# Weights and weight sums of the first up tiles made during the output projection of a diffusion layer

## The chip, the cores and the metric

The kernel runs on one core of a Trainium2 chip. The metric is the device time of one execution in microseconds (us); the time of a kernel is the median of its runs. The engines of the core are named as in the profile: PE (matrix products), DVE (vector), ACT (scalar functions and copies), POOL (GpSimd, elementwise work here) and SP (its queue issues the loads and stores).

## What is computed

One layer of a transformer for 128 context tokens and 512 latent tokens, model width 1024. The stretch that matters runs from the end of the mixer to the first up tiles of the channel sub-layer:

```python
x = x + ga * _merge(pool, na, gp, gn, w_pool_proj, w_na_proj, w_o)   # ends with (...) @ w_o
h = _modulated_norm(x, norm_ffn_g, sf, cf)
x = x + gf * _conv_ffn(h, w_up, ffn_conv_w, ffn_conv_b, w_down)

def _conv_ffn(h, w_up, conv_w, conv_b, w_down):
    u = h @ w_up
    up = jnp.pad(u, ((0, 0), (1, 1), (0, 0)))
    u = up[:, :-2] * conv_w[0] + up[:, 1:-1] * conv_w[1] + up[:, 2:] * conv_w[2] + conv_b
    a, g = jnp.split(u, 2, axis=-1)
    return (jax.nn.silu(a) * g) @ w_down
```

## The kernel before

**Arithmetic.** Every float32 operand of a product is split into a rounded high part and a remainder (split_to, L132: a cast on ACT, a subtraction on DVE), and each product is made of three matmuls, high by high, high by low and low by high. A weight tile is loaded into a buffer named raw (three of them, L125), and split into one of two pairs whi and wlo of the pool wp (L138).

**Output projection.** The mixer's result stands as mhi and mlo for five token tiles of 128. The first half of the 1024 columns is made for all five tiles at once (L718 to L722), the second half tile by tile (out_product, L730), from weights w1h and w1l that are split beforehand. residual (L708) then multiplies by the gate on DVE (L711, into one of two buffers o_t), adds to x1 (first half on POOL, L713; second half on DVE, L715) and sums the squares on ACT (L716). After the second half of a tile, out_product takes the root (L744), scales the row to xn (L747; two buffers xn2) and hands xn to second_h (L753): eight transposes on PE into small PSUM tiles sm, four modulated copies on ACT and four on DVE into hf (L764, L767), and the split into b1h, b1l, b12h, b12l, b2h, b2l. The program asks for the transposes of a tile in the middle of the next tile's out_product.

**Up projection.** It uses sums of quarters of weights and of h (seven products in place of eight). sums (L787) makes the sums of h on DVE for a range of columns J; split_sums (L796) splits them into th and tl; POOL makes the four sums of a weight tile (L859 to L862) in a buffer ws. Tile f = 0 is done without sums, by plain (L899), from the weights w0. For each later f, up_a makes two products from plain weights, up_w splits the weight sums, and products_b (L877, called in up_b) makes the other five products. up_a and up_w of tile f + 1 stand around up_b of tile f.

**Order.** A scheduler orders the instructions of each engine when the program is built: among those that it takes to be ready it prefers what stands earlier in the program. Each engine then runs its own list strictly in that order, waiting where data is late. Pools opened at L814 and L817 (tp, fw) take the memory of mhi, mlo, w1h and w1l, and so can be written only when the last output product is over. In the program the stretch ends like this:

```python
    w0a, rg = load_w(A["wup"][0]), load_raw(A["wup"][NF])
    ...                         # output projection; sums J[0] after tile 3, J[1] after tile 4
    hi, lo = [fw.tile([P, 1024], F32R, tag=x, name=x, bufs=1) for x in ("whi2", "wlo2")]
    split_to(rg, hi, lo)
    plain(B11, B21, HB, 1)
    second_h(4, xns[4])
    up_a(1)
    plain(B12, B22, H2C, 1 + HB)
    sums(*J[2])
```

B11 and B21 are the columns 0 to 321 of h, which end inside token tile 2; B12 and B22 are the rest, which need tile 4.

Of the kernel before, what the change touches and what calls it, by code (L numbers as in the profile page):

```python
# [10 lines left out]
F32 = mybir.dt.float32  # L11
F32R = mybir.dt.float32r
# [5 lines left out]
P = 128  # L18
D = 1024
# [45 lines left out]
def body(ctx, tc, A):  # L65
# [58 lines left out]
    def load_raw(src, tp=None):  # L124
        r = (tp or wp).tile([P, 1024], F32, tag="raw", name="raw", bufs=SRAW if tp else 3)  # L125
        dma = nc.sync.dma_start(r, src)
        if tp or pinned[0] > 0:
            tc.keep_in_program_order(dma)
            pinned[0] -= 0 if tp else 1
        return r  # L130

    def split_to(raw, hi, lo):  # L132
        nc.scalar.copy(hi, raw)  # L133
        nc.vector.tensor_tensor(out=lo, in0=raw, in1=hi.bitcast(F32), op=SUB)  # L134
# [297 lines left out]
    def to_grid_order(fn, ctx_dst, lat_dst, ps):  # L432
# [3 lines left out]
        fn(d[:, 0:3], blocks(ps[0][:, SEQ:320]))  # L436
        fn(d[:, 3:8], blocks(ps[1][:, :320]))

    def tanh_half(dst, src):
        i = nc.scalar.activation(dst, src, AF.Tanh, scale=0.5).ins  # L440
# [210 lines left out]
    def merge(i):  # L651
# [13 lines left out]
        nc.scalar.activation(mh, ta, AF.Copy, scale=0.5)  # L665
        nc.vector.scalar_tensor_tensor(out=ml, in0=ta, scalar=0.5, in1=mh.bitcast(F32), op0=MULT, op1=SUB)

    for i in range(KT):
        merge(i)
        for _ in range(2):  # L670
            next(mods, None)
        if i + 5 < KT:
            t2s[i + 5] = gate_na(i + 5)
# [34 lines left out]
    def residual(ps, t, chunk, sq):  # L708
        sl = slice(chunk * 512, (chunk + 1) * 512)
        tmp = fp.tile([P, 512], F32, name="o_t", bufs=2)  # L710
        nc.vector.tensor_tensor(out=tmp, in0=ps, in1=gab[:, 1 if t == 0 else 0, sl], op=MULT)  # L711
        if chunk == 0:
            nc.gpsimd.tensor_tensor(out=x1[:, t, sl], in0=x1[:, t, sl], in1=tmp, op=ADD)  # L713
        else:
            nc.vector.tensor_tensor(out=x1[:, t, sl], in0=x1[:, t, sl], in1=tmp, op=ADD)  # L715
        nc.scalar.activation(tmp, x1[:, t, sl], AF.Square, accum_out=sq[:, t:t + 1])  # L716
# [13 lines left out]
    def out_product(t, mid):  # L730
        ps = ps_acc()
        for kt in range(KT):
            if kt == MID and t:
                mid(t - 1)
            xh, xl = mhi[:, kt, tok_cols(t)], mlo[:, kt, tok_cols(t)]
            nc.tensor.matmul(ps, lhsT=xh, rhs=w1h[:, kt, :], start=(kt == 0), stop=False)
            nc.tensor.matmul(ps, lhsT=xh, rhs=w1l[:, kt, :], start=False, stop=False)
            nc.tensor.matmul(ps, lhsT=xl, rhs=w1h[:, kt, :], start=False, stop=(kt == KT - 1))
        residual(ps, t, 1, sq1)

        nc.sync.dma_start(xscr[:, t, :], x1[:, t, :])
        std = fp.tile([P, 1], F32, name="std2", bufs=2)
        nc.vector.tensor_tensor(out=std, in0=sq0[:, t:t + 1], in1=sq1[:, t:t + 1], op=ADD)
        nc.scalar.activation(std, std, AF.Sqrt, bias=eps, scale=1.0 / D)  # L744
        nc.vector.reciprocal(std, std)
        xn = fp.tile([P, D], F32, name="xn2", bufs=2)
        nc.scalar.activation(xn, x1[:, t, :], AF.Copy, scale=std)  # L747
        return xn

# [37 lines left out]
    def sums(j0, j1):  # L787

        b11, b21 = hf[:, 0:4, j0:j1], hf[:, 4:8, j0:j1]
        b12, b22 = hf[:, 0:4, HB + j0:HB + j1], hf[:, 4:8, HB + j0:HB + j1]  # L790
        nc.vector.tensor_tensor(out=b11, in0=b12, in1=b11, op=SUB)
        nc.vector.tensor_tensor(out=b12, in0=b22, in1=b12, op=SUB)
        nc.vector.tensor_tensor(out=b22, in0=b22, in1=b11, op=SUB)
        nc.vector.tensor_tensor(out=b21, in0=b21, in1=b22, op=SUB)
# [7 lines left out]
    J = ((0, 64), (64, 192), (192, HB))  # L802


    w0a, rg = load_w(A["wup"][0]), load_raw(A["wup"][NF])
    xns = []
    for t in range(5):
        xns.append(out_product(t, lambda t: second_h(t, xns[t])))
        if t >= 3:
            sums(*J[t - 3])  # L810
    e5.close()
    ex.close()
    e6 = ExitStack()
# [26 lines left out]
    def halves_of(w):  # L840
        return [tuple(x[:, i * 512:(i + 1) * 512] for x in w) for i in range(2)]
# [2 lines left out]

    def up_a(f):

        ra, rg = load_raw(A["wup"][f]), load_raw(A["wup"][NF + f])
        a11, a12, a21, a22 = ra[:, :512], ra[:, 512:], rg[:, :512], rg[:, 512:]
        hi, lo = [wp.tile([P, 1024], F32R, tag=x, name=x, bufs=2) for x in ("whi", "wlo")]
# [8 lines left out]
        s = fw.tile([P, 4, 512], F32, name="ws", bufs=1)  # L858
        nc.gpsimd.tensor_tensor(out=s[:, 1], in0=a21, in1=a22, op=ADD)  # L859
        nc.gpsimd.tensor_tensor(out=s[:, 0], in0=s[:, 1], in1=a11, op=SUB)  # L860
        nc.gpsimd.tensor_tensor(out=s[:, 2], in0=a11, in1=a21, op=SUB)
        nc.gpsimd.tensor_tensor(out=s[:, 3], in0=a12, in1=s[:, 0], op=SUB)  # L862
        ups[f] = pa, s, a22

    def up_w(f):

        pa, s, a22 = ups.pop(f)
        w = []
        for tp_, src, n in ((fw, s[:, 0:2].rearrange("p a b -> p (a b)"), 1024),
                            (wp, s[:, 2:4].rearrange("p a b -> p (a b)"), 1024), (fw, a22, 512)):  # L870
            e = "" if tp_ is wp else "2" if n == 1024 else "3"
            hi, lo = [tp_.tile([P, n], F32R, tag=x + e, name=x + e, bufs=2 if tp_ is wp else 1) for x in ("whi", "wlo")]
            split_to(src, hi, lo)
            w += halves_of((hi, lo)) if n == 1024 else [(hi, lo)]
        ups[f] = pa, w

# [15 lines left out]
        nc.scalar.copy(ug[:, h1], pa[:, cs])  # L892


    hi, lo = [fw.tile([P, 1024], F32R, tag=x, name=x, bufs=1) for x in ("whi2", "wlo2")]
    split_to(rg, hi, lo)
    w0 = [halves_of(w0a), halves_of((hi, lo))]

    def plain(x1_, x2_, n, c0):  # L899
        for (wa, wb), u in zip(w0, (us["a"][0], us["g"][0])):  # L900
# [3 lines left out]
            nc.scalar.copy(u[:, c0:c0 + n], ps[:, :n])  # L904

    plain(B11, B21, HB, 1)
    second_h(4, xns[4])
    up_a(1)
    plain(B12, B22, H2C, 1 + HB)
    sums(*J[2])  # L910
    for j in ((0, 192), (192, HB)):
        split_sums(*j)
    up_w(1)
# [206 lines left out]
```

## Time and profile before

| what | us |
|---|---|
| median of three runs | 908.28 |
| lowest and highest run | 905.41 and 909.32 |
| profiled execution, its own time | 908.53 |
| span of the profiled execution | 906.7 |
| PE busy in the span | 869.7 |
| DVE busy in the span | 669.9 |
| ACT busy in the span | 394.6 |
| POOL busy in the span | 232.9 |

The span runs from the first to the last instruction; the profiled time is 1.8 us longer. All places in the trace are given in us from the start of the span. The last output product ends near 450, and the up projection fills the rest of the span.

### The profile page before, as it was taken

Reading aid. Unit: us, or ns where it says so; the run is one execution under the profiler, and the core shown is the slowest. Engines: PE = TensorE matmul, PEld = TensorE weight load, DVE = VectorE, ACT = ScalarE, POOL = GpSimd, SP = SyncE. Lnnn points to the kernel's source line nnn. Section 1 sums busy time; section 2 is a strip of 40 time slices with the busy share of each in tenths; the row PEclk is TensorE's granted clock in tenths of the full one; section 3 lists DMA queues with packets and bytes.
Section 4 is the critical chain, followed back from the end, with each engine's and each line's share of the span. In section 5 each row is a group of like instructions: output and inputs, shape, how many; then the busy total and the mean of one; then the engine's idle time right before and its main releaser. Section 6 shows DMA issues by size and latency. Waiting matters only on the chain.

```text
span 906.7 us, 13346 instructions
## 1 busy us (share of the span) xinstructions
PE 869.7 (96%) x5234; PEld 781.0 (86%) x5234; DVE 669.9 (74%) x1000; ACT 394.6 (44%) x710; POOL 232.9 (26%) x179
## 2 busy tenths in 40 slices
PE   4999999999999999999979999999999999999997
PEld 3778897887889999987779898999999899999885
DVE  3656987897489633545699978879797887979767
ACT  5342245445453322224766444526354353544540
POOL 2220000000000021322115543354342345433304
PEclk9999999999999999999989999999999999999999
DMA  9958326573364222254123322212232221322206
GB/s 265 323 211 249 114 76 206 177 232 116 97 207 157 78 80 74 70 215 172 79 92 105 117 70 93 94 47 93 70 117 68 73 93 47 106 83 93 94 0 198
DMA packets 33023, 112.20 MB, mean 124 GB/s; under 512 B 3856, under 2 KB 4528, under 8 KB 32704
## 3 DMA queue, kind: packets, MB, share of 16 engines
q1 hardware_dynamic: 31840, 107.91, 35.8%
q0 software_dynamic: 1120, 3.44, 1.3%
q8 instruction: 41, 0.67, 0.3%
q14 instruction: 22, 0.18, 0.1%
HBM read 104.50 MB, written 5.78 MB: 122 GB/s over the span
## 4 chain that ended last, share of the span: by engine, by line
PE 77%; DVE 9%; DMA 7%; ACT 3%; issue 2%; POOL 1%; SPq 0%; DVEq 0%; ACTq 0%; POOLq 0%
PE acc L837 23%; PE acc L219 21%; PE sm L964 4%; PE sm L966 4%; PE sm L965 4%; PE acc L203 3%; PE acc L205 3%; PE acc L204 3%; DVE wlo L134 2%; ACT whi L133 2%; DMA raw<-in_wo 2%; DMA na<-in_xl 2%; DVE cv L924 1%; DMA raw<-in_wdn 1%; PE sm L541 1%
## 5 line engine op out<-in xcount | busy, mean ns | idle before, releaser
L133 ACT CAST whi<-raw 128x1024 fp32r<-128x1024 f32 (+1 forms) x86 | 81.2, 945 | 193.6 <-PE acc L837 77.0
L134 DVE TENSOR_TENSOR wlo<-raw,whi 128x1024 fp32r<-128x1024 f32 (+1 forms) x86 | 102.7, 1195 | 39.7 <-ACT whi L133 39.1
L837 PE MATMUL acc<-th,whi 128*128 128x322 f32 (+1 forms) x336 | 103.8, 313 | 4.2 <-ACT whi L133 2.2
L837 PE MATMUL acc<-tl,whi 128*128 128x322 f32 (+1 forms) x336 | 104.5, 311 | 0.0
L837 PE MATMUL acc<-th,wlo 128*128 128x322 f32 (+1 forms) x336 | 104.0, 311 | 0.0
L219 PE MATMUL acc<-hhi,whi 128*128 128x320 f32 x320 | 92.3, 322 | 0.4 <-ACT t L440 0.4
L219 PE MATMUL acc<-hlo,whi 128*128 128x320 f32 x320 | 90.1, 315 | 0.0
L219 PE MATMUL acc<-hhi,wlo 128*128 128x320 f32 x320 | 89.3, 315 | 0.0
L859 POOL TENSOR_TENSOR ws<-raw 128x512 f32<-128x512 f32 x21 | 30.7, 1462 | 176.5 <-DVE wlo L134 105.1
L965 PE MATMUL sm<-dlo,ahi 128*128 128x512 f32 (+1 forms) x188 | 74.0, 393 | 0.0
L964 PE MATMUL sm<-dhi,ahi 128*128 128x512 f32 (+1 forms) x188 | 71.4, 395 | 2.2 <-ACT dhi L133 1.7
L966 PE MATMUL sm<-dhi,alo 128*128 128x512 f32 (+1 forms) x188 | 71.4, 394 | 0.0
L837 PEld LDWEIGHTS acc<-th,whi 128*128 128x128 f32 x336 | 63.1, 189 | 8.0 <-ACT whi L133 4.4
L837 PEld LDWEIGHTS acc<-tl,whi 128*128 128x128 f32 x336 | 63.4, 189 | 1.4
L837 PEld LDWEIGHTS acc<-th,wlo 128*128 128x128 f32 x336 | 63.3, 189 | 1.2
L133 ACT CAST whi<-ws 128x1024 fp32r<-128x1024 f32 x42 | 43.1, 1047 | 42.6 <-PE acc L837 40.6
L219 PEld LDWEIGHTS acc<-hhi,whi 128*128 128x128 f32 x320 | 58.9, 193 | 2.8 <-issue 1.5
L837 PE MATMUL acc<-b1l,whi 128*128 128x322 f32 x184 | 57.6, 315 | 3.8 <-DVE b1l L134 3.8
L978 DVE TENSOR_TENSOR acc<-sm,acc 128x512 f32<-128x512 f32 x80 | 53.1, 682 | 9.2 <-PE sm L966 9.2
L219 PEld LDWEIGHTS acc<-hlo,whi 128*128 128x128 f32 x320 | 58.8, 192 | 0.8 <-issue 0.7
L219 PEld LDWEIGHTS acc<-hhi,wlo 128*128 128x128 f32 x320 | 58.2, 191 | 0.7 <-issue 0.5
L837 PE MATMUL acc<-b1h,whi 128*128 128x322 f32 x184 | 57.2, 314 | 0.9 <-ACT b1h L133 0.9
(294 smaller groups left out, 2251.3 us busy)
## 6 DMA issues: line engine op xcount, KB each, us to landing
raw<-in_wup SPq DMA_DIRECT2D x44, 512.0 KB, 3.9
mw<-in_wmT SPq DMA_DIRECT2D x32, 512.0 KB, 4.2
raw<-in_wdn SPq DMA_DIRECT2D x22, 512.0 KB, 3.5
raw<-in_wmt SPq DMA_DIRECT2D x20, 512.0 KB, 3.5
raw<-in_wm SPq DMA_DIRECT2D x16, 512.0 KB, 5.1
raw<-in_wtok SPq DMA_DIRECT2D x12, 512.0 KB, 7.6
bias<-in_bias SPq DMA_DIRECT2D x16, 384.0 KB, 4.0
raw<-in_wab SPq DMA_DIRECT2D x8, 512.0 KB, 3.5
```

The lines of the kernel that those rows point to most:

```text
L133: nc.scalar.copy(hi, raw)
L134: nc.vector.tensor_tensor(out=lo, in0=raw, in1=hi.bitcast(F32), op=SUB)
L203: nc.tensor.matmul(ps[t], lhsT=xh, rhs=wh, start=(kt == 0), stop=False)
L204: nc.tensor.matmul(ps[t], lhsT=xh, rhs=wl, start=False, stop=False)
L205: nc.tensor.matmul(ps[t], lhsT=xl, rhs=wh, start=False, stop=(kt == KT - 1))
L219: nc.tensor.matmul(o[:, :n], lhsT=w[:, k], rhs=cut(x, k, c, n), start=st and a, stop=sp and b)
L837: upped[0] = nc.tensor.matmul(ps[:, cs], lhsT=a[:, c], rhs=b[:, k, cs], start=start and first, stop=last, skip_group_check=skip and not st ...
L859: nc.gpsimd.tensor_tensor(out=s[:, 1], in0=a21, in1=a22, op=ADD)
L964: nc.tensor.matmul(ps, lhsT=xh, rhs=hi[:, sl], start=first and j == js[0], stop=False)
L965: nc.tensor.matmul(ps, lhsT=xh, rhs=lo[:, sl], start=False, stop=False)
L966: nc.tensor.matmul(ps, lhsT=xl, rhs=hi[:, sl], start=False, stop=last and j == js[-1])
L978: nc.vector.tensor_tensor(out=o, in0=ps, in1=o, op=ADD)
```

## The change

Two things are made earlier. The second weight tile of f = 0 is split at once with load_w, into the second wp pair, and so up_a(1) takes whi2 and wlo2 of fw for its own split. The weight sums of f = 1 are made on POOL ahead of the tile loop, in a buffer ws of the pool fp; later tiles keep one in fw. To make room, xn2 has one buffer.

Around that, second_h of tile 4 is asked for right after the loop, ahead of sums J[1], which move behind plain(B11, B21). The first-half addition of residual is made on DVE for tiles 0 to 2. A root of one element, ordered behind the last tanh, is made during the merges, so that the table of roots is loaded there. The split of A22 for f = 1 stays behind the DVE split before it. The first and third weight sum of f = 2 wait for the last sum of h of J[2].

```diff
+    def root_table():
+        tc.add_manual_dep(nc.scalar.activation(warm, eps, AF.Sqrt).ins, tanhs[0].name, ...)
     for i in range(KT):
         merge(i)
+        if i + 4 == KT:
+            root_table()
...
-        if chunk == 0:
+        if chunk == 0 and t > 2:
             nc.gpsimd.tensor_tensor(out=x1[:, t, sl], in0=x1[:, t, sl], in1=tmp, op=ADD)
...
-        xn = fp.tile([P, D], F32, name="xn2", bufs=2)
+        xn = fp.tile([P, D], F32, name="xn2", bufs=1)
...
-    w0a, rg = load_w(A["wup"][0]), load_raw(A["wup"][NF])
+    w0 = [load_w(A["wup"][0]), load_w(A["wup"][NF])]
+
+    def weight_sums(tp_, ra, rg, behind=None):
+        a11, a12, a21, a22 = ra[:, :512], ra[:, 512:], rg[:, :512], rg[:, 512:]
+        s = tp_.tile([P, 4, 512], F32, name="ws", bufs=1)
+        first = nc.gpsimd.tensor_tensor(out=s[:, 1], in0=a21, in1=a22, op=ADD).ins
+        nc.gpsimd.tensor_tensor(out=s[:, 0], in0=s[:, 1], in1=a11, op=SUB)
+        third = nc.gpsimd.tensor_tensor(out=s[:, 2], in0=a11, in1=a21, op=SUB).ins
+        nc.gpsimd.tensor_tensor(out=s[:, 3], in0=a12, in1=s[:, 0], op=SUB)
+        if behind:
+            for i in (first, third):
+                tc.add_manual_dep(i, behind.name, ...)
+        return a22, s
+
+    ra, rg = load_raw(A["wup"][1]), load_raw(A["wup"][NF + 1])
+    summed = (ra, *weight_sums(fp, ra, rg))
     xns = []
     for t in range(5):
         xns.append(out_product(t, lambda t: second_h(t, xns[t])))
-        if t >= 3:
-            sums(*J[t - 3])
+        if t == 3:
+            sums(*J[0])
+    second_h(4, xns[4])
...
+        if f == 1:
+            hi, lo = [fw.tile([P, 1024], F32R, tag=x, name=x, bufs=1) for x in ("whi2", "wlo2")]
+        else:
+            hi, lo = [wp.tile([P, 1024], F32R, tag=x, name=x, bufs=2) for x in ("whi", "wlo")]
...
+        if f > 1:
+            a22, s = weight_sums(fw, ra, rg, summed_h if f == 2 else None)
...
-            split_to(src, hi, lo)
+            i = split_to(src, hi, lo)
+            if f == 1 and n == 512:
+                tc.keep_in_program_order(i)
...
-    hi, lo = [fw.tile([P, 1024], F32R, tag=x, name=x, bufs=1) for x in ("whi2", "wlo2")]
-    split_to(rg, hi, lo)
-    w0 = [halves_of(w0a), halves_of((hi, lo))]
+    w0 = [halves_of(w) for w in w0]
...
     plain(B11, B21, HB, 1)
-    second_h(4, xns[4])
+    sums(*J[1])
     up_a(1)
     plain(B12, B22, H2C, 1 + HB)
-    sums(*J[2])
+    summed_h = sums(*J[2])
```

## Rows read from the trace of the kernel before

**Rows 1.** The page, part 1: busy us of each engine, its share, instructions.
```profile
PE 869.7 (96%) x5234; PEld 781.0 (86%) x5234; DVE 669.9 (74%) x1000; ACT 394.6 (44%) x710; POOL 232.9 (26%) x179
```

**Rows 2.** Busy time by stretch: length, PE, PEld, DVE, ACT, POOL (instructions), PE clock, DMA.
```profile
419.30:450.30 31.00, 30.70 (x149) 25.24 (x147) 18.26 (x38) 20.51 (x43) 6.38 (x5) 1.00 0.23 88
450.30:454.76 4.46, 2.03 (x12) 1.20 (x10) 4.46 (x6) 4.44 (x11) 4.39 (x9) 1.00 0.29 118
454.76:461.59 6.83, 3.00 (x12) 2.86 (x12) 6.83 (x14) 3.07 (x7) 2.59 (x2) 0.50 0.70 230
461.59:483.00 21.41, 21.09 (x141) 20.29 (x141) 19.88 (x32) 15.92 (x27) 1.38 (x1) 1.00 0.09 25
483.00:506.00 23.00, 20.42 (x134) 19.58 (x134) 22.16 (x18) 12.90 (x19) 16.80 (x10) 1.00 0.37 125
```

**Rows 3.** Timeline of PE: start, length, line, tiles, count [idle before, releaser].
```profile
452.26 0.66 PE L759 MATMUL sm<-ident,xn 128*128 128x128 f32 x4 [1.58 <-ACT hf L764]
453.25 0.71 PE L837 MATMUL acc<-b1h,whi 128*128 128x322 f32 x3 [0.34 <-ACT b1h L133]
454.48 0.42 PE L837 MATMUL acc<-b1h,whi 128*128 128x322 f32 x1 [0.52 <-ACT b1h L133]
458.73 0.64 PE L837 MATMUL acc<-b1l,whi 128*128 128x322 f32 x1 [3.83 <-DVE b1l L134]
...
478.95 0.31 PE L837 MATMUL acc<-b1h,whi 128*128 128x322 f32 x1
...
482.81 0.31 PE L837 MATMUL acc<-th,whi 128*128 128x322 f32 x1
```

**Rows 4.** Timeline of DVE: the work ahead of b1l, in its order.
```profile
452.34 2.30 DVE L134 TENSOR_TENSOR wlo<-raw,whi 128x1024 fp32r<-128x1024 f32 x1
454.55 1.75 DVE L134 TENSOR_TENSOR wlo<-raw,whi 128x512 fp32r<-128x512 f32 x1
456.23 1.48 DVE L791 TENSOR_TENSOR hf<-hf 128x256 f32<-128x256 f32 x1
458.27 0.41 DVE L134 TENSOR_TENSOR b1l<-hf,b1h 128x256 fp32r<-128x256 f32 x1
```

**Rows 5.** Timeline of POOL: the last weight sum of f = 1, the first of f = 2.
```profile
455.83 1.59 POOL L862 TENSOR_TENSOR ws<-raw,ws 128x512 f32<-128x512 f32 x1
481.62 1.84 POOL L859 TENSOR_TENSOR ws<-raw 128x512 f32<-128x512 f32 x1 [24.20 <-DVE wlo L134]
```

**Rows 6.** Timeline of DVE: the same kinds of operations later, and the conv.
```profile
460.60 0.41 DVE L792 TENSOR_TENSOR hf<-hf 128x256 f32<-128x256 f32 x1
477.15 0.69 DVE L134 TENSOR_TENSOR tl<-hf,th 128x520 fp32r<-128x520 f32 x1
480.26 1.22 DVE L134 TENSOR_TENSOR wlo<-ws,whi 128x1024 fp32r<-128x1024 f32 x1
481.42 0.89 DVE L924 SCALAR_TENSOR_TENSOR cv<-ua,vec,cv 128x642 f32<-128x642 f32 x1
482.23 1.92 DVE L924 SCALAR_TENSOR_TENSOR cv<-ug,vec,cv 128x642 f32<-128x642 f32 x1
```

**Rows 7.** Groups of POOL, 419 to 429: the first-half additions of residual.
```profile
L713 POOL TENSOR_TENSOR x<-x,o_t 128x512 f32<-128x512 f32 x5 | 6.4, 1293 | 25.0 <-DMA raw<-in_wup 22.9 <-DVE o_t L711 2.1
```

**Rows 8.** Timeline of ACT: root table, casts and xn of tiles 1 and 4.
```profile
429.85 1.28 ACT L744 ACT_TABLE_LOAD   x1
434.52 1.15 ACT L747 ACTIVATE xn<-x,std 128x1024 f32<-128x1024 f32 x1 [0.23 <-DVE std L745]
...
461.87 1.15 ACT L747 ACTIVATE xn<-x,std 128x1024 f32<-128x1024 f32 x1
...
477.38 1.05 ACT L133 CAST whi<-raw 128x1024 fp32r<-128x1024 f32 x1 [0.71 <-PE acc L837]
```

**Rows 9.** Timeline of DVE: the start of tile 1's second residual.
```profile
431.55 0.67 DVE L711 TENSOR_TENSOR o_t<-acc,gab 128x512 f32<-128x512 f32 x1
```

**Rows 10.** What PE waited for, 459 to 520: total us, times, longest.
```profile
PE sm L964 <- ACT dhi L133: 1.7, 1, 1.7
```

More of the change, by code (lines that the diff above doesn't have):

```diff
@@ L133, in split_to @@
         nc.scalar.copy(hi, raw)
-        nc.vector.tensor_tensor(out=lo, in0=raw, in1=hi.bitcast(F32), op=SUB)
+        return nc.vector.tensor_tensor(out=lo, in0=raw, in1=hi.bitcast(F32), op=SUB)
     def load_w(src, own=None):
@@ L437, in to_grid_order @@
         fn(d[:, 3:8], blocks(ps[1][:, :320]))
+    tanhs = [None]
     def tanh_half(dst, src):
-        i = nc.scalar.activation(dst, src, AF.Tanh, scale=0.5).ins
+        i = tanhs[0] = nc.scalar.activation(dst, src, AF.Tanh, scale=0.5).ins
         tc.add_manual_dep(i, roots[-1].name,
@@ L666, in merge @@
         nc.vector.scalar_tensor_tensor(out=ml, in0=ta, scalar=0.5, in1=mh.bitcast(F32), op0=MULT, op1=SUB)
+    def root_table():
+        tc.add_manual_dep(nc.scalar.activation(warm, eps, AF.Sqrt).ins, tanhs[0].name,
+                          mybir.DependencyInfo(mybir.DependencyClass.NoSync, mybir.DependencyReason.DATA),
+                          reason="one table after the other")
     for i in range(KT):
         merge(i)
+        if i + 4 == KT:
+            root_table()
         for _ in range(2):
@@ L793, in sums @@
         nc.vector.tensor_tensor(out=b22, in0=b22, in1=b11, op=SUB)
-        nc.vector.tensor_tensor(out=b21, in0=b21, in1=b22, op=SUB)
+        return nc.vector.tensor_tensor(out=b21, in0=b21, in1=b22, op=SUB).ins
     def split_sums(j0, j1):
@@ L802, in body @@
     J = ((0, 64), (64, 192), (192, HB))
-    w0a, rg = load_w(A["wup"][0]), load_raw(A["wup"][NF])
+    w0 = [load_w(A["wup"][0]), load_w(A["wup"][NF])]
[8 more added lines that the diff above has]
+            for i in (first, third):
+                tc.add_manual_dep(i, behind.name,
+                                  mybir.DependencyInfo(mybir.DependencyClass.Sync, mybir.DependencyReason.DATA),
+                                  reason="behind the sums of h2")
+        return a22, s
+    ra, rg = load_raw(A["wup"][1]), load_raw(A["wup"][NF + 1])
+    summed = (ra, *weight_sums(fp, ra, rg))
     xns = []
@@ L845, in up_a @@
     def up_a(f):
-        ra, rg = load_raw(A["wup"][f]), load_raw(A["wup"][NF + f])
-        a11, a12, a21, a22 = ra[:, :512], ra[:, 512:], rg[:, :512], rg[:, 512:]
-        hi, lo = [wp.tile([P, 1024], F32R, tag=x, name=x, bufs=2) for x in ("whi", "wlo")]
+        if f == 1:
+            ra, a22, s = summed
+        else:
+            ra, rg = load_raw(A["wup"][f]), load_raw(A["wup"][NF + f])
+        if f == 1:
+            hi, lo = [fw.tile([P, 1024], F32R, tag=x, name=x, bufs=1) for x in ("whi2", "wlo2")]
+        else:
+            hi, lo = [wp.tile([P, 1024], F32R, tag=x, name=x, bufs=2) for x in ("whi", "wlo")]
         split_to(ra, hi, lo)
@@ L857, in up_a @@
         nc.vector.tensor_tensor(out=us["a"][f % 2][:, 1:1 + HB], in0=pb[:, :HB], in1=p1, op=ADD)
[L858 to L862, printed above, removed]
+        if f > 1:
+            a22, s = weight_sums(fw, ra, rg, summed_h if f == 2 else None)
         ups[f] = pa, s, a22
```

## The prediction

> **What bounds the kernel now.** The page first: PE is busy in 869.7 of 906.7 us, all other engines far less [rows 1]. A kernel like that is shortened where PE stands still, so the next view is busy time by stretch. In the second half of the output projection PE works 30.70 of 31.00 us; from 450.30 to 461.59 it works 2.03 + 3.00 of 11.29 us, while DVE has no idle time at all; after that PE is full again up to 483 [rows 2]. The third view is PE's timeline in that hole. Four waits: 1.58 us for a small PSUM tile that ACT empties late, 0.34 and 0.52 us for b1h, and 3.83 us for b1l of token tile 2 [rows 3]. Together 6.27 us. The fourth view is DVE's list ahead of that b1l: a weight split of 2.30 us (the second weight tile of f = 0), one of 1.75 us (A22 of f = 1) and a sum of h of 1.48 us [rows 4]. None of these is needed by the matmul that waits. They stand there because their buffers come free, or their data, just as the last output product ends.
>
> They are also slow. POOL makes the sums of f = 1 beside them: it is busy 4.39 of the first 4.46 us of the hole [rows 2], and the last sum ends at 455.83 + 1.59 = 457.42 [rows 5]. In that time the split of 1024 columns takes 2.30 us against 1.22 later, and the sum of 256 columns 1.48 against 0.41 [rows 4, 6]; the split of 512 takes 1.75, where 520 columns take 0.69 in a split of tl [rows 4, 6]. That is 3 x 1.1 = 3.3 us.
>
> The hole has a second price. From 454.76 to 461.59 the granted clock is 0.50, the 1.2 GHz level, after PE had worked little since 450.3 [rows 2]. Eleven of its twelve matmuls run from 458.73 [rows 3] to its end, 2.86 / 11 = 0.26 us each, against 21.41 / 141 = 0.15 us in the next stretch [rows 2]: 11 x 0.11 = 1.2, with the first one's delay some 1.3 us. So 6.27 + 1.3 = 7.6 us hang on this place.
>
> **The change part by part.**
>
> *Split of f = 0's second weight.* It moves into the second wp pair, which up_a(1)'s split takes now during the projection; up_a(1)'s split moves into whi2 and to the hole. DVE's count there stays, but what waits for it does not: up_a(1) comes after the 48 matmuls of plain, 48 x 0.15 = 7.2 us. At nothing in the projection, where DVE is busy 18.26 and ACT 20.51 of 31 us [rows 2]; if that cover failed, PE would see one split of 1.22 us. The loads of the four up tiles keep their number and order.
>
> *Weight sums of f = 1.* Four POOL operations of about 1.3 us leave the hole and with them the 3.3 us of DVE time. They land on the projection behind two raw tiles, next to POOL's additions for tiles 3 and 4 (queued on the same engine, 1.29 us each [rows 7]), which ACT's squares and then the two o_t buffers wait for. The cover is PE's own list, which has output products without waits up to 450; an accumulator is asked for again only after 24 matmuls of its successor. Without the cover a tile comes one or two operations, 1.3 to 2.6 us, later.
>
> *Three additions on DVE, one root early, one xn buffer.* Per addition 1.29 - 0.69 = 0.6 us less in the chain of o_t (0.69 is the tl split of 520 columns [rows 6], a DVE operation of the same kind and size), and the 1.28 us table load [rows 8] leaves tile 0's chain. So h of the early tiles is ready some 2 to 3 us sooner; PE has no wait there now, so this pays only by having tile 2 split before 450. The single xn buffer makes each xn wait for the transposes of the tile before; those are out_products apart. Nothing on the path; bound 0 to 0.5 us. The early root costs ACT the same 1.28 us and the root itself among the merges; on the page ACT is busy in 44% of the span [rows 1].
>
> *A22's split held back.* 0.69 us (1.75 now) leave DVE's list in the hole. Its product is the last of five in products_b(1). It holds a raw buffer longer, and with it the load for f = 3 that waits for that buffer on SP's list, and whatever SP has behind that load. The sums of f = 3 cannot start before those of f = 2 are split, so nothing waits for that load yet; without that cover the price is one weight split, 1.22 us. I count nothing.
>
> *Transposes of tile 4 asked for early, sums J[1] later.* xn of tile 4 ends at 463.02 now [rows 8] because its small operations queue on DVE. Tile 1's chain, from the multiplication at 431.55 [rows 9] to the end of xn at 435.67 [rows 8], took 4.1 us with little in its way; so xn(4) can end at 450.3 + 4.1 = 454.4, while PE has 7.2 + 24 x 0.15 = 10.8 us of plain and up_a(1). Nothing, if PE's list has the transposes behind some of these.
>
> What stays or comes in, then. (a) *Rest of the hole.* Between 0 and 2.4 us (the three smaller waits, 1.58 + 0.34 + 0.52); I take 0.5, close to the 0.34 and 0.52 waits, since the casts that held ACT are fewer. (b) *up_a(2)'s weights.* Now they are cast at 477.38, when the first w0 pair is free, and up_a(2) starts at 478.95 [rows 3, 8]. After the change both wp pairs hold w0 and the first one to come free goes to the sums of f = 1, so the split of up_a(2) starts when the second half of plain is over: 1.05 + 1.22 = 2.3 us with nothing else to run, 0 if products_b(1) can go first, which needs all of T2. I take 0.8, nearer to the end where other work is ready. (c) *Sums of f = 2 beside split_sums.* POOL is nearly idle up to 481.62 now (1.38 of 21.41 us [rows 2]), since the one ws buffer holds f = 1's sums [rows 5]. With a buffer of their own, the sums of f = 2 start behind J[2], while DVE makes tl and weight splits. A DVE operation beside a POOL sum took 1.92 us against 0.89 [rows 6], so four sums cost DVE 4 x 1.0 = 4.1 us, and the conv is spared as much. For PE that is 0 as long as th and tl are ahead of it: the third of four tl pieces ended at 477.84 [rows 6] and the first th product came at 482.81 [rows 3], 5 us of slack, but PE now arrives some 6 us sooner, and DVE sooner by its 3.3 us and by what it does before 450. Between 0 and 4.1; I take 0.5, near the present slack.
>
> Here a rule speaks against the change. The Trainium skill, SBUF — State Buffer, section Who interferes with whom, says that a DVE instruction with two inputs in SBUF and a GpSimd instruction that reads SBUF exclude each other for a whole instruction. The rows agree in kind: about 1.1 us added per operation. By that rule the change moves the collision rather than removing it, from a place with PE idle to one with DVE nearly full.
>
> (d) *Further on.* PE waits 1.7 us for the first down weights shortly before 506 [rows 10]. Their loads wait for raw buffers, which all change hands earlier or later by a few us. That wait could go or double; I count 0, bounds -1.7 and +1.7.
>
> Sum: -6.27 - 1.3 + 0.5 + 0.8 + 0.5 = -5.8. From the profiled 908.53, which is 0.25 above the median, this gives 902.7.
>
> **The rivals.**
>
> *Half done (904.7).* The scheduler still puts up_a(1)'s split ahead of tile 2's b1l. For it: the same kind of split stood there, released by the same memory. Against it: tile 2 gets earlier. Then b1l ends 3.3 + 0.7 us sooner (no POOL beside it, no A22), so the 3.83 us wait and the 1.3 us of slow clock go, the other 2.4 stay: -5.1 + 0.8 + 0.5.
>
> *DVE becomes the bound (906.3).* (c) at its full 4.1 us: -7.6 + 0.5 + 0.8 + 4.1 = -2.2. For it: DVE is full from 450 to 506 now (22.16 of 23.00 in the last stretch [rows 2]). Against: it loses 3.3 us of stretched work first, and part of tile 2's and 3's work to the time before 450.
>
> *Short stall at the transposes (905.6).* PE's list has tile 4's transposes right behind tile 3's. The last four of tile 3 take 0.66 us [rows 3], so PE is through at about 451.0 and waits to 454.4: 3.4 us, so -7.6 + 3.4 + 0.8 + 0.5 = -2.9.
>
> *Long stall at the transposes (914.2).* The same place, and xn(4) still ends at 463.0 as now. PE stands 12.0 us and meets the slow clock again: -6.27 + 12.0 = +5.7. What decides is the end of xn(4): later than 451.0 + 6.3 = 457.3 and the kernel is slower than before. Against it: tile 4's small operations now stand ahead of J[1]'s sums in the program, and the scheduler passes over what it does not take to be ready, which xn(4) cannot be at 451.
>
> *All of it (below 901).* (a) to (c) near 0, and perhaps the wait of (d) gone too: 908.53 - 7.6 = 900.9, down to 899.2.
>
> **How the numbers follow.** Forecast 0.50, its own range 901 to 904.5; half done 0.15; DVE bound 0.13; short stall 0.07; long stall 0.08; all of it 0.07. The range 899.2 to 907.8 takes in all but the long stall and the far ends of the others (DVE's term of 4.1 us with the wait of (d) grown by 1.7 would be 908.0). A change of 0.5% (4.5 us, about what a measurement of this kernel can tell) lies at 903.7 and 912.8. Faster: four fifths of the forecast, the best case, a third of half done and some of the rest, 0.55. Slower: nearly the long stall alone, 0.07. Within: 0.38.
>
> **What would show it.** PE's waits between 450 and 462 sum to about 0.5 us and no stretch there is at 0.50 clock. No POOL sum lies there; DVE's b1l of tile 2 ends before 451. The weight sums of f = 1 lie between 422 and 432 with PE still above 30 of 31 us. xn(4) ends near 455 and its transposes stand inside plain or up_a(1). Waits before up_a(2) or the first th product: about 1.3 us; more than 3 there means that DVE is the bound. The forecast is wrong if PE waits for xn(4), or if the clock falls again.

## The result, and the profile after

The changed kernel takes 905.85 us in the median of 20 runs (901.14 to 909.41), the kernel before 909.94 us in 20 runs beside it (905.30 to 915.76). The ratio is 0.9950 with a 95% interval of 0.9933 to 0.9967: 4.1 us faster. Measured a second time it gave 907.31 against 910.20 us, 0.9964 (0.9944 to 0.9983): 3.3 us by the ratio. The forecast was 5.8. The profiled execution took 904.50 us, with a span of 902.7.

The page of the changed kernel, part 1: busy us, share, instructions. It answers to [rows 1].

```profile
PE 864.6 (96%) x5234; PEld 778.1 (86%) x5234; DVE 663.9 (74%) x1003; ACT 394.3 (44%) x711; POOL 227.1 (25%) x176
```

PE, DVE and POOL are each busy 5 to 6 us less. PE has the same matmuls, and DVE has even three additions more, so the operations themselves were shorter. For PE the mean granted clock, 0.992 before and 0.995 here, accounts for at most 2.7 us of the 5.1; where the rest comes from was not followed up.

Places need an anchor. The first output product starts at 418.25 here, at 419.93 in the kernel before. These 1.7 us can't be put down to the change: the same changed kernel has its first output product at 421.00 in its second profile, and in the profiles below it lies anywhere from 416.01 to 423.56. So places are also given as us after the first output product.

Busy time of each engine by stretch, columns as in [rows 2]: the rest of the output projection with the waits behind it, the first products of plain, the stretch up to up_a(2), and the stretch of the first down products.

```profile
418.25:450.30 32.05, 30.22 (x145) 25.00 (x145) 20.53 (x41) 19.15 (x42) 8.33 (x12) 1.00 0.27 99
450.30:457.27 6.97, 5.46 (x24) 4.81 (x25) 6.71 (x20) 6.97 (x18) 0.00 (x0) 0.76 0.49 150
457.27:479.57 22.30, 20.60 (x142) 20.33 (x141) 21.43 (x28) 15.13 (x27) 7.24 (x4) 1.00 0.12 39
480.00:506.00 26.00, 23.23 (x149) 22.18 (x149) 23.30 (x25) 15.98 (x23) 11.37 (x6) 1.00 0.40 137
```

Timeline of PE in the same places, columns as in [rows 3]: every wait over 0.25 us from 418 to 506, the eight transposes of tile 4 (at 458.80) and the first th product (at 473.55).

```profile
450.30 0.66 PE L768 MATMUL sm<-ident,xn 128*128 128x128 f32 x4 [1.83 <-ACT xn L756]
451.95 0.66 PE L768 MATMUL sm<-ident,xn 128*128 128x128 f32 x4 [1.00 <-ACT hf L773]
453.12 1.18 PE L865 MATMUL acc<-b1h,whi 128*128 128x322 f32 x4 [0.52 <-ACT b1h L133]
...
458.80 1.03 PE L768 MATMUL sm<-ident,xn 128*128 128x128 f32 x8
...
473.55 0.31 PE L865 MATMUL acc<-th,whi 128*128 128x322 f32 x1
...
479.57 0.41 PE L865 MATMUL acc<-b1h,wlo 128*128 128x322 f32 x1 [1.70 <-DVE wlo L134]
...
499.51 0.97 PE L994 MATMUL sm<-dhi,ahi 128*128 128x512 f32 x3 [2.48 <-ACT dhi L133]
500.77 0.50 PE L995 MATMUL sm<-dlo,ahi 128*128 128x512 f32 x1 [0.29 <-DVE dlo L134]
```

Beside [rows 3] three things are to be seen. The wait of 3.83 us for b1l is gone, and POOL does nothing from 450.30 to 457.27. But three waits stand at the end of the projection again, 1.83 + 1.00 + 0.52 = 3.35 us, and the largest has a new cause: xn, not hf. And there are waits at two places that are new or larger: 1.70 us at up_a(2), whose high part is ready and whose low part (wlo) is late, and 2.48 + 0.29 us at the first down weights [rows 10].

Two lists show what stands ahead of xn of tile 3. POOL's, in the projection:

```profile
422.30 1.79 POOL L819 TENSOR_TENSOR ws<-raw 128x512 f32<-128x512 f32 x1 [26.84 <-DMA raw<-in_wup]
424.07 1.30 POOL L821 TENSOR_TENSOR ws<-raw 128x512 f32<-128x512 f32 x1
425.33 1.28 POOL L820 TENSOR_TENSOR ws<-ws,raw 128x512 f32<-128x512 f32 x1
426.58 1.28 POOL L722 TENSOR_TENSOR x<-x,o_t 128x512 f32<-128x512 f32 x1
427.83 1.30 POOL L822 TENSOR_TENSOR ws<-raw,ws 128x512 f32<-128x512 f32 x1
429.08 1.28 POOL L722 TENSOR_TENSOR x<-x,o_t 128x512 f32<-128x512 f32 x1
```

And ACT's: the square that waits for POOL, the two casts ahead of tile 3's xn (x2: one of 1024 columns and one of 512), and xn of tiles 0, 1, 3 and 4.

```profile
427.90 0.63 ACT L725 ACTIVATE o_t<-x 128x512 f32<-128x512 f32 x1 [4.15 <-POOL x L722]
...
432.77 1.16 ACT L756 ACTIVATE xn<-x,std 128x1024 f32<-128x1024 f32 x1 [0.23 <-DVE std L754]
435.69 1.15 ACT L756 ACTIVATE xn<-x,std 128x1024 f32<-128x1024 f32 x1 [0.29 <-DVE std L754]
...
447.63 1.56 ACT L133 CAST whi<-raw 128x1024 fp32r<-128x1024 f32 x2 [0.56 <-PE acc L747]
449.10 1.15 ACT L756 ACTIVATE xn<-x,std 128x1024 f32<-128x1024 f32 x1
...
454.24 1.16 ACT L756 ACTIVATE xn<-x,std 128x1024 f32<-128x1024 f32 x1
```

Three weight sums are ahead of POOL's addition for tile 3 and a fourth is ahead of that for tile 4. ACT's square waits 4.15 us, and both o_t buffers wait with it. Tile 1's xn ends at 435.69 + 1.15 = 436.84, which is 18.6 us after the first output product; before it was 15.7 [rows 8]. Tile 3's xn stands behind two more things, the single buffer and ACT's two casts. Which of them PE's wait comes from, the experiments ask.

### The profile page after: what moved, and what is told of

The parts are those of the page before. It is cut to its first block, busy times and chain, and to the rows that moved or that the text cites. A ratio compares the mean times of both kernels' runs of the same rounds, so it can differ in the third digit from the quotient of the medians.

```text
span 902.7 us, 13356 instructions
## 1 busy us (share of the span) xinstructions
PE 864.6 (96%) x5234; PEld 778.1 (86%) x5234; DVE 663.9 (74%) x1003; ACT 394.3 (44%) x711; POOL 227.1 (25%) x176
## 4 chain that ended last, share of the span: by engine, by line
PE 82%; DVE 7%; DMA 5%; ACT 3%; issue 2%; SPq 0%; POOL 0%; DVEq 0%; ACTq 0%; POOLq 0%
PE acc L865 25%; PE acc L219 21%; PE sm L995 5%; PE sm L996 5%; PE sm L994 4%; PE acc L203 4%; PE acc L205 4%; PE acc L204 4%; DVE wlo L134 2%; DMA raw<-in_wdn 2%; DMA na<-in_xl 2%; ACT whi L133 2%; PE sm L543 1%; PE sm L527 1%; PE sm L505 1%
## 5 line engine op out<-in xcount | busy, mean ns | idle before, releaser
L134 DVE TENSOR_TENSOR wlo<-ws,whi 128x1024 fp32r<-128x1024 f32 x42 | 51.6, 1248 | 8.2 <-ACT whi L133 8.2
```

The lines of the kernel that those rows point to most:

```text
L134: return nc.vector.tensor_tensor(out=lo, in0=raw, in1=hi.bitcast(F32), op=SUB)
```

## The experiments

The theory had three parts. First, xn of tile 3 is held by the single xn2 buffer: it must wait for the transposes of tile 2, and PE's list has those behind the last output product (447.43). One rival was POOL's list, which made tiles 0 to 2 late; another was ACT's two casts of weights, which stand ahead of tile 3's work. Second, the 1.70 us at up_a(2) come from the sums of f = 2 beside DVE. The rival was that the added wait of POOL behind the sums J[2] costs it. Third, the gain comes from the early weights and not from the new order around tile 4.

The table sums PE's waits by place in the one profiled execution of each kernel (columns in us after the first output product: the end of the projection with the last transposes and the first halves, then up to the products of B12, then up to up_a(2) and the products behind it, then up to the first down weights). "Slow" is what stretches at 0.50 clock cost up to the first th product: there the starts of the up projection's matmuls are 0.27 us apart in place of 0.15, so half of the distances between the starts, waits left out, is counted, which is a little too much. In the kernel before, the 3.83 us for b1l fall into the second column.

| kernel | ratio to before (95%) | 29 to 36 | 36 to 58 | 58 to 70 | 70 to 90 | slow | sum |
|---|---|---|---|---|---|---|---|
| before | 1 | 2.43 | 4.11 | 0.65 | 1.98 | 1.43 | 10.6 |
| after | 0.9950 (0.9933 to 0.9967) | 3.35 | 0 | 1.70 | 2.77 | 1.48 | 9.3 |
| after_again | 0.9964 (0.9944 to 0.9983) | 2.88 | 0 | 1.70 | 3.14 | 2.85 | 10.6 |
| two_xn | 0.9939 (0.9912 to 0.9965) | 2.23 | 2.97 | 0 | 2.12 | 1.68 | 9.0 |
| x_first | 0.9975 (0.9954 to 0.9996) | 2.83 | 0.97 | 0.29 | 3.65 | 2.71 | 10.5 |
| no_wait | 0.9964 (0.9939 to 0.9989) | 3.34 | 2.70 | 0 | 1.87 | 3.08 | 11.0 |
| later_sums | 0.9940 (0.9918 to 0.9962) | 3.34 | 0 | 0.45 | 1.84 | 1.48 | 7.1 |
| combo2 | 0.9962 (0.9944 to 0.9980) | 2.43 | 1.02 | 0 | 2.86 | 0 | 6.3 |
| combo4 | 0.9959 (0.9936 to 0.9982) | 2.21 | 2.97 | 0.48 | 1.85 | 1.60 | 9.1 |
| weights_only | 0.9985 (0.9960 to 1.0011) | 4.02 | 4.20 | 0 | 1.72 | 4.17 | 14.1 |
| order_only | 0.9978 (0.9955 to 1.0001) | 2.43 | 3.22 | 1.18 | 1.40 | 2.50 | 10.7 |
| order_back, order_back2 | 0.9978 (0.9958 to 0.9998) | 3.34 | 0.62 | 0.30 | 3.28 | 1.47 | 9.0 |

The sums, of one execution each, do not rank the ratios: weights_only has 14.1 us and combo2 6.3, and their intervals overlap.

**after_again.** The changed kernel once more.

> The changed kernel once more, for a second profile. If the stalls seen in its first profile belong to it: the same waits of PE within 0.3 us (1.83 and 1.00 at the transposes of tile 3, 0.52 at b1h, 1.70 before up_a(2)'s low part, 2.48 at the first down weights), and 484 to 485 us from the first output product to the end of the span. If the two extra stretches at 0.50 clock that the first profile of the kernel before had ahead of the output projection are chance, such stretches stand at other places here. Ratio to before 0.993 to 0.997.

0.9964. The waits of 1.83 and 1.00 us at the transposes and of 1.70 at up_a(2) repeat to within 0.01 us. The 0.52 us for b1h are gone, the waits for the first down weights are 2.85 + 0.30, and the stretch at 0.50 clock behind the transposes was twice as long, 6.8 us against 3.4. From the first output product to the end of the span it took 487.67 us, not 484 to 485.

**two_xn.** The xn of odd tiles has a place of its own, a row that is no longer needed:

```diff
-        xn = fp.tile([P, D], F32, name="xn2", bufs=1)
+        xn = x1[:, t - 1, :] if t % 2 else fp.tile([P, D], F32, name="xn2", bufs=1)
```

> xn of the odd tiles goes into the row of x1 of the tile before, which is dead by then, so that xn has two buffers again without more memory. Theory: the 1.83 and 1.00 us at tile 3's transposes come from the single buffer, since xn(3) has to wait for the transposes of tile 2 and those for PE; then transposes 2 and 3 move back among the output products, PE's waits from the last output product to the twelfth product of plain fall from 3.35 to under 1 us and no stretch at 0.50 clock stands there: 3 to 4.5 us less than the changed kernel, ratio to before 0.990 to 0.992. Rival: the casts of weights (1.05 and 0.61 us) that ACT does first when the pool comes free hold tile 3 in any case; then the same waits only move to b1h or b1l and the time stays within 1 us of the changed kernel.

ACT's xn of tiles 3 and 4, and PE's waits:

```profile
444.54 1.15 ACT L756 ACTIVATE x<-x,std 128x1024 f32<-128x1024 f32 x1
455.35 1.16 ACT L756 ACTIVATE xn<-x,std 128x1024 f32<-128x1024 f32 x1
```

```profile
450.08 0.70 PE L865 MATMUL acc<-b1h,whi 128*128 128x322 f32 x3 [1.45 <-ACT b1h L133]
451.56 0.41 PE L865 MATMUL acc<-b1l,whi 128*128 128x322 f32 x1 [0.78 <-DVE b1l L134]
465.14 0.57 PE L865 MATMUL acc<-b12h,whi 128*128 128x320 f32 x2 [2.21 <-ACT b12h L133]
466.47 0.63 PE L865 MATMUL acc<-b12l,whi 128*128 128x320 f32 x1 [0.76 <-DVE b12l L134]
```

Its first output product starts at 417.36, so xn of tile 3 ends at 445.69, 28.3 us after it; with one buffer it ended 32.0 after it. The transposes of tile 2 are back between output products; those of tile 3 follow the last one, as in the kernel before. The waits at the end of the projection fall from 3.35 to 2.23, not below 1: ACT's two casts now stand ahead of the halves, and PE waits for b1h and b1l. The rival of the casts came true in that part. Tile 4's xn ends 39.1 us after the first output product in place of 37.2, and PE waits 2.97 us for tile 4's halves. What was won at one place was asked back at the next; the ratio is not to be told from that of the changed kernel. So the buffer does hold xn of tile 3, and with two places PE waits 1.1 us less here.

**x_first.** POOL's two additions are ordered ahead of the weight sums of f = 1:

```diff
+            added[0] = nc.gpsimd.tensor_tensor(out=x1[:, t, sl], in0=x1[:, t, sl], in1=tmp, op=ADD).ins
...
+        if tp_ is fp:
+            for i in (first, third):
+                tc.add_manual_dep(i, added[0].name, ...)
```

> On POOL's list the weight sums of f = 1 stand behind the additions of residual for tiles 3 and 4, in place of ahead of and between them. Theory: in the changed kernel these two additions ended at 427.9 and 430.4 because sums were ahead, so that DVE stood still for 4.2 us at an o_t buffer and xn of tile 0 came 14.5 us after the first output product (11.7 before the change); with the additions first xn of tile 0 comes 2.5 to 4 us sooner, and of PE's 3.35 us of waits at tile 3's transposes and b1h at least 1.5 go: 1.5 to 3 us below the changed kernel, ratio to before 0.992 to 0.994. Rival: the single xn buffer ties xn(2) and xn(3) to the transposes, which PE's list has where it had them, and the waits stay: within 0.7 us.

Timelines of ACT (xn of tiles 0 and 3) and of PE:

```profile
430.82 1.15 ACT L758 ACTIVATE xn<-x,std 128x1024 f32<-128x1024 f32 x1 [0.23 <-DVE std L756]
...
451.80 1.15 ACT L758 ACTIVATE xn<-x,std 128x1024 f32<-128x1024 f32 x1
```

```profile
453.00 0.66 PE L770 MATMUL sm<-ident,xn 128*128 128x128 f32 x4 [1.83 <-ACT xn L758]
454.64 1.11 PE L770 MATMUL sm<-ident,xn 128*128 128x128 f32 x4 [0.99 <-ACT hf L775]
```

The first output product starts at 420.93, so xn of tile 0 ends 11.0 us after it, 4.6 earlier than in the changed kernel (433.93 - 418.25 = 15.7), and xn of tile 3 still ends 32.0 after it. The waits of 1.83 and 1.00 us stand as they were, and the ratio, 0.9975, is no better. So POOL's list delays the early tiles, but that is not what PE waits for here: the rival falls. What this run leaves as the cause is the buffer together with the two casts, which end at 450.32 + 1.56 = 451.88, just where xn of tile 3 starts. In the changed kernel the transposes that free the buffer end at 448.46 and xn starts at 449.10, behind the casts. The first part of the theory holds for xn of tile 3, and for 1.1 us of the waits (two_xn).

**no_wait.** POOL's wait behind the sums J[2] is taken out; up to the first down products every engine's list of instructions stays as it is:

```diff
-            a22, s = weight_sums(fw, ra, rg, summed_h if f == 2 else None)
+            a22, s = weight_sums(fw, ra, rg, None)
```

> The weight sums of f = 2 no longer wait for the last sum of h; the order on every engine stays. Theory (DVE nearly the bound): the sums start when their raw tile has landed, near 455, and stretch the sums and splits of h by about 1 us each, so th and tl come 2 to 4 us later and PE waits before the first th product or before b12l: 1 to 3 us slower than the changed kernel. Rival: DVE has slack at 455 to 470 and none at 472 to 479, so that the 1.70 us wait before up_a(2)'s low part, whose split took 2.29 us beside POOL, goes and nothing takes its place: 1 to 2 us faster.

The 1.70 us at up_a(2) are gone, and 2.20 + 0.49 us for b12h and b12l stand before the products of B12. The sums of f = 2 ran some 36 to 44 us after the first output product, beside DVE's work on tile 4. The added wait does what it is there for: it keeps POOL off that work, and moves the price, from 2.70 to 1.70 us in these profiles. The ratios, 0.9964 here and in after_again, show no difference.

**later_sums.** The sums of f = 2 are held back further, behind the low part of up_a(2)'s split:

```diff
-        split_to(ra, hi, lo)
+        split = split_to(ra, hi, lo).ins
...
-            a22, s = weight_sums(fw, ra, rg, summed_h if f == 2 else None)
+            a22, s = weight_sums(fw, ra, rg, split if f == 2 else None)
```

> The weight sums of f = 2 wait for the low part of up_a(2)'s split in place of the last sum of h. Theory: the 1.70 us wait before up_a(2)'s low part comes from four DVE operations of 1.49, 1.77, 1.79 and 2.29 us beside POOL, which take 3.8 us without it; then that wait is at most 0.3 us, the conv operations behind it are stretched as before the change (1.9 us in place of 0.9), and the kernel is 1 to 2 us below the changed one unless the first down weights take it back. Rival: DVE is full in any case and PE waits for the silu chain or the down weights by as much more: within 0.5 us.

DVE's same four operations ahead of up_a(2), in the changed kernel and then in this one:

```profile
472.40 1.49 DVE L134 TENSOR_TENSOR wlo<-ws,whi 128x1024 fp32r<-128x1024 f32 x1 [0.75 <-ACT whi L133]
473.81 1.77 DVE L134 TENSOR_TENSOR wlo<-raw,whi 128x512 fp32r<-128x512 f32 x1
475.51 1.79 DVE L134 TENSOR_TENSOR tl<-hf,th 128x520 fp32r<-128x520 f32 x1
477.22 2.29 DVE L134 TENSOR_TENSOR wlo<-raw,whi 128x1024 fp32r<-128x1024 f32 x1
479.44 0.88 DVE L954 SCALAR_TENSOR_TENSOR cv<-ua,vec,cv 128x642 f32<-128x642 f32 x1
```

```profile
475.91 1.23 DVE L134 TENSOR_TENSOR wlo<-ws,whi 128x1024 fp32r<-128x1024 f32 x1 [0.76 <-ACT whi L133]
477.05 0.69 DVE L134 TENSOR_TENSOR wlo<-raw,whi 128x512 fp32r<-128x512 f32 x1
477.65 0.69 DVE L134 TENSOR_TENSOR tl<-hf,th 128x520 fp32r<-128x520 f32 x1
478.26 1.22 DVE L134 TENSOR_TENSOR wlo<-raw,whi 128x1024 fp32r<-128x1024 f32 x1
479.43 0.89 DVE L954 SCALAR_TENSOR_TENSOR cv<-ua,vec,cv 128x642 f32<-128x642 f32 x1
480.24 1.90 DVE L954 SCALAR_TENSOR_TENSOR cv<-ug,vec,cv 128x642 f32<-128x642 f32 x1
```

PE's only wait over 0.15 us from 460 to 500 in this kernel:

```profile
488.67 0.42 PE L865 MATMUL acc<-th,wlo 128*128 128x322 f32 x1 [0.45 <-DVE wlo L134]
```

The four take 7.34 us beside POOL and 3.83 us without it: the four sums cost DVE 3.5 us. The wait at up_a(2) is gone whole. The collision is not: the conv pays now, with 1.90 to 1.92 us in place of 0.88 for three of its four operations, and so does the next split of weight sums, with 2.36 us; the new wait of 0.45 us, 66.9 us after the first output product in place of 61.3, is for that split. PE reads the conv's results much later. This settles the second part.

**combo2 and combo4.** Repairs together: combo2 has all three, combo4 has two_xn with later_sums. Their edits are those above.

> Two xn buffers (odd tiles in dead rows of x1), the additions of tiles 3 and 4 ahead of the weight sums on POOL, and the sums of f = 2 behind up_a(2)'s split. Theory: each takes one wait away (tile 3's transposes and xn, 2 to 3 us; tile 0's chain; up_a(2)'s low part, 1.7 us), so that PE waits under 1.5 us from the last output product to the first down weights, without a stretch at 0.50 clock: 4 to 6 us below the changed kernel, ratio to before 0.989 to 0.991. Rival: DVE's total work between 447 and 480 is the bound, and waits taken from one place come back at the next (as with two xn buffers alone): 1 to 2 us below the changed kernel, 0.993 to 0.995.

> The changed kernel with two repairs at once: xn of odd tiles in a second place, and the sums of f = 2 behind the low part of up_a(2)'s split. If the waits found so far are independent, the hole of PE falls from 3.35 to about 2.2 us and the 1.70 us before up_a(2) go, while the 2.97 us before plain(B12) that the second xn alone brought stay: some 904 to 906, a ratio to the kernel before of 0.993 to 0.995. If what ends these waits is DVE's full list from 447 to 480, the repairs do not add: the wait before plain(B12) or at the down weights grows by what the others lose, and the ratio stays at 0.995 to 0.996. A ratio under 0.992 would say that both repairs add in full.

In combo2 PE loses 6.3 us in the places of the table, the least of all kernels. The wait at up_a(2) is gone, but 1.31 us stand at the first product of up_a(3), 70.1 us after the first output product. And the end of the projection has the three waits of the kernel before again (PE, then ACT's casts):

```profile
453.04 0.65 PE L770 MATMUL sm<-ident,x 128*128 128x128 f32 x4 [1.57 <-ACT hf L775]
454.03 0.71 PE L872 MATMUL acc<-b1h,whi 128*128 128x322 f32 x3 [0.34 <-ACT b1h L133]
455.26 0.41 PE L872 MATMUL acc<-b1h,whi 128*128 128x322 f32 x1 [0.52 <-ACT b1h L133]
```

```profile
451.06 1.56 ACT L133 CAST whi<-raw 128x1024 fp32r<-128x1024 f32 x2 [0.36 <-PE acc L749]
```

In combo4 the repairs each do what they did alone, 2.21 at the end of the projection and 0.48 behind up_a(2), and the 2.97 us of two_xn stay. Neither ratio is better than that of the changed kernel or of later_sums; the intervals overlap widely. Differences of 2 to 3 us in these places are below what the runs resolve: the intervals are some 2 us to each side, and the two profiles of the changed kernel alone differ by 3.2 us in what the slow clock cost behind the first output product.

**weights_only.** Early split and early sums with the single xn buffer; the additions, the early root, the order around tile 4, the held split of A22 and POOL's wait are as in the kernel before:

```diff
-        if chunk == 0 and t > 2:
+        if chunk == 0:
...
-        if t == 3:
-            sums(*J[0])
-    second_h(4, xns[4])
+        if t >= 3:
+            sums(*J[t - 3])
...
-    sums(*J[1])
+    second_h(4, xns[4])
```

> Only the early split, the early weight sums and the buffers that they need, with the single xn; the additions on POOL, the root where it was, tile 4 and J[1] as before the change, no pin and no wait. Theory: this part alone takes the 3.83 us wait for b1l and its stretched splits away, but five additions now queue with four sums on POOL, so tile 0 comes later than in the changed kernel: PE's waits from 447 to 455 come to 3.5 to 6 us, and the time lies between both kernels, ratio to before 0.996 to 0.999. Rival: the small parts do nothing and this is as fast as the changed kernel: 0.995 to 0.9965.

Timeline of PE:

```profile
448.74 0.66 PE L766 MATMUL sm<-ident,xn 128*128 128x128 f32 x4 [2.51 <-ACT xn L754]
450.91 1.11 PE L766 MATMUL sm<-ident,xn 128*128 128x128 f32 x4 [1.51 <-ACT hf L771]
...
468.65 0.90 PE L862 MATMUL acc<-b12h,whi 128*128 128x320 f32 x2 [4.14 <-ACT b12h L133]
```

0.9985, not to be told from no change. With all five additions on POOL among the four sums, tile 0's xn ends 18.0 us after the first output product, the waits at the transposes are 4.02 us, and 4.14 us for b12h come in place of the 3.83 us for b1l. In its profile the early weights alone only trade one wait for another.

**order_only.** The complement: additions on DVE, early root, tile 4 ahead of J[1], A22 held, with the weights as in the kernel before:

```diff
-    w0 = [load_w(A["wup"][0]), load_w(A["wup"][NF])]
+    w0a, rg = load_w(A["wup"][0]), load_raw(A["wup"][NF])
...
-    summed = (ra, *weight_sums(fp, ra, rg))
...
+    hi, lo = [fw.tile([P, 1024], F32R, tag=x, name=x, bufs=1) for x in ("whi2", "wlo2")]
+    split_to(rg, hi, lo)
```

> The rest of the change without the early weights: three additions on DVE, the early root, tile 4's transposes ahead of the sums J[1] and the split of A22 held back, while the second weight's split and the sums of f = 1 stay in the hole as in the kernel before. By the prediction these parts are worth little alone (POOL's sums keep DVE slow in the hole, and the 3.83 us wait for b1l stays): 907 to 910, ratio 0.998 to 1.001. By the rival, that the order carries the gain: the sum of PE's waits from 29 to 58 us after the first output product is 4 us or less, against 6.5 in the kernel before and 3.35 in the changed one, and the ratio is 0.994 to 0.997.

Timeline of PE:

```profile
455.87 0.66 PE L768 MATMUL sm<-ident,xn 128*128 128x128 f32 x4 [1.58 <-ACT hf L773]
...
461.09 0.64 PE L847 MATMUL acc<-b1l,whi 128*128 128x322 f32 x1 [2.58 <-DVE b1l L134]
475.86 0.41 PE L847 MATMUL acc<-b12l,whi 128*128 128x320 f32 x1 [0.53 <-DVE b12l L134]
```

The wait for b1l falls from 3.83 to 2.58 us and no further: the split of A22 is out of its way, but POOL's sums still run beside it, and the other split, still 2.29 us long, stands ahead of it. 0.9978, with an interval that reaches no change. Against the third part of the theory: neither half alone gives a gain that the runs can tell from nothing, and both together give 0.995 to 0.9964. Whether 1.4 and 2.0 us add up to the whole or fall short of it can't be told with intervals of some 2 us to each side.

**order_back and order_back2.** The changed kernel with the sums J[1] ahead of tile 4's transposes, as before:

```diff
-        if t == 3:
-            sums(*J[0])
-    second_h(4, xns[4])
+        if t >= 3:
+            sums(*J[t - 3])
+    second_h(4, xns[4])
...
-    sums(*J[1])
```

> Only the place of second_h of tile 4 and of the sums J[1] in the program is as before; everything else as in the changed kernel. The transposes of tile 4 then stand behind 50 products of plain and up_a(1) in place of 26. Theory: h of tile 4 comes 3 to 4 us later, and so do its sums and splits; PE waits 2 to 4 us more before the first th products or before up_a(2)'s low part, and the time is 2 to 4 us above the changed kernel. Rival: DVE is full anyway and only the order of its work differs: within 1 us.

> One look at the changed kernel with the h2 sums J[1] ahead of tile 4's transposes as before. If the new place of the transposes costs and brings nothing, PE's waits from 29 to 58 us after the first output product stay near 3.35 us. If it is what lets xn of tile 4 end early, xn of tile 4 ends 3 us or more later than in the changed kernel (36 us after the first output product), and a wait of some us for its halves b12h and b12l stands before plain(B12).

order_back gave 0.9978 (0.9958 to 0.9998), which overlaps with after_again of the same occasion. order_back2 is the same kernel, and its trace is the one that is read. On its ACT the xn of tile 4 is this line:

```profile
453.87 1.15 ACT L756 ACTIVATE xn<-x,std 128x1024 f32<-128x1024 f32 x1
```

It ends 37.1 us after the first output product (417.88), in the changed kernel 37.2 us after it. So it is not the new place of J[1] that makes tile 4 early. PE waits 0.62 us more up to B12 and 1.40 us less at up_a(2): no cost and no gain that could be shown.

## Why the prediction was right in direction and too high in size

**What held.** The hole was read rightly: the 3.83 us for b1l came from POOL's sums and two early splits, and went with them, in weights_only too. The split of 1024 columns took 1.22 us in place of 2.30 [rows 4]:

```profile
448.95 1.22 DVE L134 TENSOR_TENSOR wlo<-raw,whi 128x1024 fp32r<-128x1024 f32 x1
```

PE still had no wait between the output products, so the weight sums were covered there. xn of tile 4 was forecast for 454.4 to 455 and ended at 454.24 + 1.16 = 455.40; its transposes found a place inside plain at no cost. The long and the short stall at the transposes did not come.

**The term that failed: (a), the rest of the hole.** It was put at 0.5 us, at most 2.4, and came to 3.35. With that the stretch at 0.50 clock stayed too: from 453.86 to 457.27, twelve matmuls, 1.5 us. That is one of the two signs by which the prediction itself would call the forecast wrong. So the hole costs 3.35 + 1.5 = 4.8 us where 0.5 was forecast, and the gain there is 7.6 - 4.8 = 2.8. Three steps of the prediction bear on it.

- "Since the casts that held ACT are fewer." They are not. The cast of f = 0's second weight left the hole, and up_a(1)'s cast of the same size took its place; A22's cast stayed, since only its split on DVE was held back. In the kernel before the two casts take 1.57 us (the line below this list), in the changed one 1.56 us at the same point of the work (447.63). combo2, with early tiles and a second place for xn, has the waits of the kernel before, 1.57 + 0.34 + 0.52 = 2.43, behind the same two casts. So 2.4 was to be expected from this step alone, not 0.5. No run takes the casts away: that they hold these waits is read from the lists, not shown.
- "The single xn buffer ... Nothing on the path; bound 0 to 0.5 us." The transposes of two tiles were said to be out_products apart. That is their place in the program; in PE's list those of tile 2 stand behind the last output product, and xn of tile 3 then runs between two groups of transposes with PE idle. two_xn shows it, with the xn 3.7 us earlier and 1.1 us less at this place; between the changed kernel and combo2 it is 3.35 - 2.43 = 0.9.
- "h of the early tiles is ready some 2 to 3 us sooner." Tile 1's xn came 2.9 us later (18.6 against 15.7), and tile 2 was not split before 450: its b1h starts at 452.66 on ACT. The text named the weight sums as neighbours of POOL's additions, priced them at 1.3 to 2.6 us, and dropped the price since PE's own list covers it, while another step counted on the same tiles being early. The step is wrong, but it is not what cost the 3.35: x_first has tile 0 earlier by 4.6 us, and the waits of 1.83 and 1.00 stay.

```profile
450.28 1.57 ACT L133 CAST whi<-raw 128x1024 fp32r<-128x1024 f32 x2 [0.39 <-PE acc L738]
```

**The terms (b) and (c)**, 0.8 + 0.5 = 1.3, came to 1.70. By later_sums all of it is (c): without POOL beside it up_a(2)'s split was ready before PE came. The price of four sums on DVE was 3.5 us against a forecast of 4.1. Here the rule of the Trainium skill (SBUF — State Buffer, Who interferes with whom) that spoke against the change was borne out in kind: the collision was moved, and PE pays 1.70 us for it in the new place. **The term (d)**, 0 with bounds of 1.7, came to 2.77 - 1.7 = 1.1. PE comes to the down products 5.3 us earlier after the first output product than before, their loads are issued only 4.6 us earlier (76.5 against 81.1), and ACT's cast of the first of them waits 3.49 us for its load, against 2.32 before.

**The rivals.** "Half done" has about the measured time, but not for its reason: a split of 1024 columns did stand ahead of tile 2's b1l, at 448.95, and b1l was not waited for. "DVE becomes the bound" is half right. DVE is busy 21.43 of 22.30 us up to up_a(2), and two_xn and no_wait show that a wait taken away at one place stands at the next where DVE's or ACT's halves of a tile are due; yet the collision at up_a(2) cost PE 1.70 us, not 4.1.

**What stays open.** By its terms the gain is 2.8 - 1.7 - 1.1 = 0, with 0.9 us of small waits, before B12 and at the products of the sums, that went too (4.11 + 0.65 - 3.83 = 0.93). The two traces differ by more: from the first output product to the end of the span 486.80 and 484.48 us, so 2.3, of which 1.2 are waits; the rest lies in neither waits nor slow clock, and what it is was not found. In the second profile of the changed kernel the same length is 487.67 us, with 3.2 us more of slow clock. The medians say 3.3 to 4.1. So two traces do not account for the whole gain. Nor does a rarer slow clock: the mean granted clock is 0.9903 over the runs of after_again and 0.9903 over those of the kernel before beside them, and yet they differ by 3.3 us. How often an execution meets later waits was not measured.

## What to carry to other kernels

A cover holds for one engine: when work is put ahead of others in a queue because the busiest engine does not notice, follow the chain that it delays to the next place where that engine will ask for it. Here the late tiles did not cost what PE waits for at that place; it took a run to tell. Work that is replaced by work of the same size on the same engine, as the cast here, has not left the place. A buffer count is checked against the list of the engine that frees the buffer, not against the program's order. And where the second engine is nearly full, a wait that is taken away can reappear, here some 6 to 15 us on; count the gain from the sum of the waits, not from the one that went.

## What the hardware showed

In the hole the granted clock falls to 0.50, the 1.2 GHz level, after PE has waited, and that adds some 1.5 us to the matmuls of a stretch of 3.4 us. Every kernel in the table has such a stretch there except two_xn, combo2 and combo4, where the waits there sum to 2.21 to 2.43 us (before and order_only have 2.43 us too, and 3.83 and 2.58 more for b1l); two_xn and combo4 have one behind their 2.97 us of waits before B12 instead. Its length varies for one and the same kernel: 3.4 us in one profile of the changed kernel, 6.8 in the other. Stretches ahead of the projection, at about 180 and 274 us, are in some executions and missing in others of kernels that are alike there.

POOL's weight sums took 1.28 to 1.30 us where DVE stood idle (4.19 us up to 428.65) and 1.61 to 2.27 us beside DVE's work ahead of up_a(2), so both sides pay: a DVE operation of 0.69 us became one of 1.77 or 1.79.
